# Down projection of a gated ConvFFN by seven block products, with weight sums formed in device memory

## The chip, the cores and the metric

One core of a Trainium2 chip runs the whole program. The engines spoken of are PE (TensorE: matmuls, and PEld for the loading of their stationary operand), DVE (VectorE), ACT (ScalarE), POOL (GpSimd) and SP (SyncE, which here only issues transfers). The metric is the time on the device in microseconds (us), the median of the runs shown; lower is better. A profile is one execution recorded by the hardware profiler.

## The reference, cut to what matters

The program is one layer of a decoder trunk, for 1024 positions of width 1024, in float32. `@` is a matrix product.

```python
h = layer_norm(x, ln_in_g, ln_in_b)
u = h @ w_in                                  # 1024 x 1024 @ 1024 x 9248
u_glu, z, xbc, dt_raw, gate_a, gate_b = split_in(u)
y_a = conformer_branch(u_glu, ...)            # depthwise conv of 31 taps, norm, product
y_b = ssd_branch(z, xbc, dt_raw, ...)         # Mamba-2 in chunks of 128 positions
mix = (sigmoid(gate_a) * y_a + sigmoid(gate_b) * y_b) @ w_o
h = layer_norm(ALPHA * h + mix, ln1_g, ln1_b)

def conv_ffn(h, w_up, dw_w, dw_b, w_down):
    u = causal_dwconv(h @ w_up, dw_w, dw_b)   # up: 1024 x 1024 @ 1024 x 5632, 3 taps
    gate, val = split(u, 2, axis=-1)          # 2816 columns each
    return (silu(gate) * val) @ w_down        # down: 1024 x 2816 @ 2816 x 1024

h = layer_norm(ALPHA * h + conv_ffn(h, ...), ln2_g, ln2_b)
```

## The kernel before

**Precision.** Each float32 operand of a large product is split into a rounded part and a remainder: `A.copy` on ACT makes the first, a subtraction on DVE the second (`weights`, L144 to L153, for a tile that comes from memory; `split_pair`, L723 to L728, for a tile at hand). A product of two split operands is three matmuls (`mm3`, L158 to L163). Weight tiles are 128 x 1024 and pass through three staging buffers (`wst`, tag "st") and three split buffers (`wsp`, tag "w"). All transfers are issued on SP, in one order that a scheduler fixes when the program is built; so is the order of each engine.

**Stages.** The positions are worked in two halves of 512 (`hh`). For each half: `ln_in`, `mixers`, `combine`, and an output projection. In `mixers(hh)` a loop over four groups `g` makes six columns of the input projection (`column`), the gate tiles `zs` (`z_gate`: four tiles, written by ACT at L443), two GLU tiles (`glu`, for which `conv31` does 30 taps each on DVE at L415), and then the chunks of 128 positions of the SSD branch (`ssd_group`). There, for each of four chunks, POOL multiplies the tile `au` at L473 into a single buffer, and two matmuls at L482 read it. So POOL can make the next `au` only when PE has read the last one, and PE goes on to the next chunk only when the next `au` is there. At the end of each half `combine` sums on POOL (L611, L613, L624).

**Up projection.** `ffn_blocks` cuts h into blocks (early and late positions, first and second half of the width) and forms sums of blocks; the product with the up weights is done as seven block products in place of eight. `up_first` does two of them for a pair of tiles and stores the results in device memory; `up_rest` does the other five for each `j` of 22. The weight sums that these need are formed on DVE in `up_weights` (four subtractions or additions of 128 x 512, L823 to L826), from two tiles loaded at L818 and L820. `up_rest` ends with the taps, the gate and a store of the activated tile (128 channels x 1024 positions) at L882.

**Down projection.** `down(hh)` takes the 22 activated tiles and the 22 weight tiles of one half of the positions: for each `k` it loads a weight tile of 128 x 1024 and an activation tile of 128 x 512, splits both, and does eight blocks of three matmuls into eight accumulators: 22 x 8 x 3 matmuls for a half and 1056 in all. The last four tiles are done position by position so that the layer norm of one (`ln_out`) runs beside the matmuls of the next.

Of the kernel before, what the change touches and what calls it, by code (L numbers as in the profile page):

```python
# [16 lines left out]
P = 128  # L17
D = 1024
# [37 lines left out]
def kernel(  # L56
# [82 lines left out]
    act_scr = [dram.tile([P, T], F32, name=f"act_scr{j}") for j in range(NF)]  # L139
# [4 lines left out]
    def weights(src, name, pl=None, eng=None, bufs=None):  # L144
# [8 lines left out]
        return w  # L153

# [400 lines left out]
    def mixers(hh, hT):  # L555
        pre = first_columns(hh, hT, (CT_DT, CT_B, CT_C))
        with pool(f"mixers{hh}") as pl:
            time_steps(pl, hh, pre[0])
            for g in range(GROUPS):
# [5 lines left out]
                zs = z_gate(pl, hh, hT, g)  # L565
                vs = [(i, glu(pl, hh, hT, i)) for i in (2 * g, 2 * g + 1)]
# [163 lines left out]
    def ffn_blocks(tp, qp, mixT):  # L730
# [33 lines left out]
        def block_sums(t):  # L764
# [9 lines left out]
            e.tensor_tensor(out=t1, in0=t0, in1=raw[:, 0:4, ts], op=ALU.subtract)  # L774
            V.tensor_tensor(out=t0, in0=b22, in1=t0, op=ALU.subtract)
            parts(lambda i: sums[0][:, i, :, ts], b22)
            V.tensor_tensor(out=t2, in0=b22, in1=t1, op=ALU.subtract)
            parts(lambda i: sums[2][:, i, :, ts], t2)
            parts(lambda i: sums[1][:, i, :, ts], t1)
            e.tensor_tensor(out=t2, in0=raw[:, 4:8, ts], in1=t2, op=ALU.subtract)  # L780
# [20 lines left out]
    def up_first(qp, bl, j):  # L801

        w = weights(wup[j], f"ue{j}")
        ps = bank(1)
        product(ps, lambda i: w[:, i, 0:HALF], bl["b11"], True)
        s1 = qp.tile([P, HALF], F32, tag="s1", bufs=2, name=f"s1_{j}")
# [3 lines left out]
        c11 = qp.tile([P, HALF], F32, tag="c11", bufs=2, name=f"c11_{j}")  # L810
        A.copy(c11, ps)
        SY.dma_start(first_scr[j][1], c11)

    def up_weights(upp, j):

        with tc.high_priority(offset=2000):
            r1 = upp.tile([P, D], F32, tag="raw", bufs=3, name=f"ra{j}")
            SY.dma_start(r1, wup[j])  # L818
            r2 = upp.tile([P, D], F32, tag="raw", bufs=3, name=f"rb{j}")
            SY.dma_start(r2, wup[NF + j])  # L820
            a11, a12, a21, a22 = r1[:, :HALF], r1[:, HALF:], r2[:, :HALF], r2[:, HALF:]
            s3 = upp.tile([P, HALF], F32, tag="s3", name=f"s3_{j}")
            V.tensor_tensor(out=s3, in0=a11, in1=a21, op=ALU.subtract)  # L823
# [5 lines left out]
            w3 = split_pair(upp, s3, f"s3_{j}", HALF, 2)  # L829
        return w24, w10, w3  # L830

    def up_rest(upp, bl, j):
# [17 lines left out]
        V.tensor_tensor(out=uv[:, late], in0=uv[:, late], in1=pc_, op=ALU.add)  # L850
# [3 lines left out]
        V.tensor_tensor(out=uv[:, 2 : 2 + HALF], in0=s, in1=pc_, op=ALU.add)  # L854
        os = []
        for jj, u in ((j, ug), (NF + j, uv)):
            o = upp.tile([P, T], F32, tag="o", bufs=2, name=f"fo{jj}")
# [24 lines left out]
        SY.dma_start(act_scr[j], ov)  # L882

    def down(upp, dp, hh, g, b):

        LAST, OWN = 4, 2
        pss = [[bank(1), bank(0)] for _ in range(4)]
        ws, acts = {}, {}
        hs = slice(hh * HALF, (hh + 1) * HALF)

        def load(k):
            own = k >= NF - OWN
            ws[k] = weights(wdown[k], f"dn{hh}_{k}", dp if own else None, bufs=OWN if own else None)
            with tc.high_priority(offset=2000):
                raw = upp.tile([P, D], F32, tag="raw", bufs=3, name=f"ar{hh}_{k}")[:, :HALF]
                SY.dma_start(raw, act_scr[k][:, hs])
                if hh == 0 and k < 2:
                    acts[k] = split_pair(upp, raw, f"act{hh}_{k}", HALF, 2)
                else:
                    acts[k] = split_pair(dp, raw, f"act{hh}_{k}", HALF, 4, "act")  # L900

        def block(k, t, q):
            mm3(
                pss[t][q],
                lambda i: acts[k][:, i, t * P : (t + 1) * P],
                lambda i: ws[k][:, i, q * HALF : (q + 1) * HALF],
                k == 0,
                k == NF - 1,
            )

        for k in range(NF - LAST):
            load(k)
            for t in range(4):
                for q in range(2):
                    block(k, t, q)
        rs = []
        for t in range(4):
            r = dp.tile([P, D], F32, tag="r", bufs=4, name=f"rf{hh}_{t}")
            SY.dma_start(r, h1_scr[(4 * hh + t) * P : (4 * hh + t + 1) * P, :])
            rs.append(r)  # L920
        for k in range(NF - LAST, NF):
            load(k)
        for t in range(4):
            for q in range(2):
                for k in range(NF - LAST, NF):
                    block(k, t, q)
                r = rs[t][:, q * HALF : (q + 1) * HALF]
                V.scalar_tensor_tensor(
# [146 lines left out]
```

## Time and profile before

| | |
|---|---|
| median of 3 runs | 2039.78 us (2038.25 to 2040.18) |
| the profiled execution, time | 2041.08 us |
| the profiled execution, span of its trace | 2039.3 us |
| granted PE clock, mean | 0.996 |
| busy: PE, PEld, DVE, ACT, POOL | 98%, 81%, 81%, 48%, 7% of the span |
| transfers | 278.24 MB on one queue, 40.3% of 16 engines |

The span runs from the first to the last instruction. A busy PE is not a PE at its peak: matmuls overlap, so the distance from one start to the next is what each costs, and not its duration. The stages of the first half of the positions lie at about 0 to 700 us, those of the second half at 700 to 1400, the up projection at 1400 to 1785 and the down projection from 1785.2 to the end. A row of the timeline has the start in us, the duration in us, the engine, the line, the operation and its tiles; "x6" are six instructions merged in one row. A row of the table of stretches has for each engine its busy us and the number of instructions, then the granted PE clock, the busy share of the transfer engines, and GB/s.

### The profile page before, as it was taken

Reading aid. Unit: us, or ns where it says so; the run is one execution under the profiler, and the core shown is the slowest. Engines: PE = TensorE matmul, PEld = TensorE weight load, DVE = VectorE, ACT = ScalarE, POOL = GpSimd, SP = SyncE. Lnnn points to the kernel's source line nnn. Section 1 sums busy time; section 2 is a strip of 40 time slices with the busy share of each in tenths; the row PEclk is TensorE's granted clock in tenths of the full one; section 3 lists DMA queues with packets and bytes.
Section 4 is the critical chain, followed back from the end, with each engine's and each line's share of the span. In section 5 each row is a group of like instructions: output and inputs, shape, how many; then the busy total and the mean of one; then the engine's idle time right before and its main releaser. Section 6 shows DMA issues by size and latency. Waiting matters only on the chain.

```text
span 2039.3 us, 24778 instructions
## 1 busy us (share of the span) xinstructions
PE 2000.0 (98%) x9296; PEld 1650.1 (81%) x9296; DVE 1654.7 (81%) x2185; ACT 973.0 (48%) x1392; POOL 148.0 (7%) x125
## 2 busy tenths in 40 slices
PE   7999999999999999999999999999999999999998
PEld 6888887888788888888888888877888888888886
DVE  7599999989766869999998976586888888853736
ACT  4465654556453356665454635354444444433231
POOL 2010101001400000100100130010000000000000
PEclk9999999999999999999999999999999999999999
DMA  6222223333436522222323353566454444464542
GB/s 218 93 69 88 86 94 104 99 103 114 158 121 213 209 88 77 90 84 76 126 88 104 109 171 128 195 217 217 155 164 157 164 165 156 160 227 149 209 159 83
DMA packets 95015, 279.81 MB, mean 137 GB/s; under 512 B 10800, under 2 KB 10800, under 8 KB 94896
## 3 DMA queue, kind: packets, MB, share of 16 engines
q1 hardware_dynamic: 94896, 278.24, 40.3%
q8 instruction: 73, 1.20, 0.2%
q14 instruction: 46, 0.38, 0.1%
HBM read 229.96 MB, written 48.23 MB: 136 GB/s over the span
## 4 chain that ended last, share of the span: by engine, by line
PE 69%; DVE 23%; issue 4%; DMA 2%; ACT 1%; SPq 0%; POOL 0%; DVEq 0%; ACTq 0%
PE acc L163 15%; PE acc L161 15%; PE acc L162 15%; DVE c L415 8%; PE sm L161 6%; PE sm L163 6%; PE sm L162 6%; DVE xbc L370 2%; PE acc L352 1%; PE sm L529 1%; PE sm L510 1%; DVE w_so L150 1%; DVE w_z L150 1%; DVE w_c L150 1%; PE sm L187 1%
## 5 line engine op out<-in xcount | busy, mean ns | idle before, releaser
L415 DVE SCALAR_TENSOR_TENSOR c<-v,pc,c 128x512 f32<-128x512 f32 x480 | 375.3, 805 | 7.2 <-ACT c L404 5.8
L473 POOL TENSOR_TENSOR au<-seg_mv,head_of 128x1024 fp32r<-128x1024 f32 x32 | 77.6, 2425 | 961.8 <-PE sm L482 728.8
L161 PE MATMUL acc<-hT,w_c 128*128 128x512 f32 x352 | 141.0, 400 | 0.0
L162 PE MATMUL acc<-hT,w_c 128*128 128x512 f32 x352 | 140.6, 399 | 0.0
L163 PE MATMUL acc<-hT,w_c 128*128 128x512 f32 x352 | 138.4, 393 | 0.0
L150 DVE TENSOR_TENSOR w_dn<-st_dn,w_dn 128x1024 fp32r<-128x1024 f32 x44 | 53.4, 1222 | 104.2 <-ACT w_dn L149 104.2
L370 DVE SCALAR_TENSOR_TENSOR xbc<-u,pc,xbc 128x512 f32<-128x512 f32 x144 | 109.8, 774 | 0.7 <-ACT xbc L368 0.5
L161 PE MATMUL sm<-h1s,w_s 128*128 128x512 f32 x264 | 103.5, 392 | 6.0 <-DVE fuv L848 3.1
L149 ACT CAST w_dn<-st_dn 128x1024 fp32r<-128x1024 f32 x44 | 46.0, 1053 | 131.6 <-PE sm L163 115.4
L162 PE MATMUL sm<-h1s,w_s 128*128 128x512 f32 x264 | 102.8, 389 | 0.0
L163 PE MATMUL sm<-h1s,w_s 128*128 128x512 f32 x264 | 102.1, 389 | 0.0
L162 PE MATMUL acc<-w_z,hT 128*128 128x512 f32 x256 | 100.8, 394 | 0.0
L161 PE MATMUL acc<-w_z,hT 128*128 128x512 f32 x256 | 100.8, 401 | 0.0
L163 PE MATMUL acc<-w_z,hT 128*128 128x512 f32 x256 | 100.7, 396 | 0.0
L149 ACT CAST w_c<-st_c 128x1024 fp32r<-128x1024 f32 x50 | 52.5, 1051 | 86.9 <-PE acc L163 66.2
L162 PEld LDWEIGHTS acc<-hT,w_c 128*128 128x128 f32 x352 | 66.1, 188 | 16.9 <-issue 3.8
L163 PEld LDWEIGHTS acc<-hT,w_c 128*128 128x128 f32 x352 | 66.1, 188 | 16.1 <-issue 2.6
L161 PEld LDWEIGHTS acc<-hT,w_c 128*128 128x128 f32 x352 | 66.1, 188 | 15.9 <-issue 2.6
L150 DVE TENSOR_TENSOR w_c<-st_c,w_c 128x1024 fp32r<-128x1024 f32 x47 | 60.6, 1289 | 20.2 <-ACT w_c L149 20.2
L163 PE MATMUL acc<-h1b,w_ue 128*128 128x512 f32 x176 | 68.5, 391 | 2.0 <-DVE w_ue L150 2.0
L161 PE MATMUL acc<-h1b,w_ue 128*128 128x512 f32 x176 | 68.7, 391 | 1.1 <-ACT s L807 0.7
L163 PE MATMUL sm<-h1b,w_s 128*128 128x512 f32 x176 | 69.2, 393 | 0.0
(312 smaller groups left out, 5741.8 us busy)
## 6 DMA issues: line engine op xcount, KB each, us to landing
st_c<-wcol SPq DMA_DIRECT2D x50, 512.0 KB, 3.5
st_dn<-wdown SPq DMA_DIRECT2D x44, 512.0 KB, 3.6
st_z<-wz SPq DMA_DIRECT2D x32, 512.0 KB, 3.4
st_wo<-wo SPq DMA_DIRECT2D x24, 512.0 KB, 3.9
st_ue<-wup SPq DMA_DIRECT2D x22, 512.0 KB, 4.1
ra<-wup SPq DMA_DIRECT2D x22, 512.0 KB, 3.8
rb<-wup SPq DMA_DIRECT2D x22, 512.0 KB, 3.5
act_scr<-fo SPq DMA_DIRECT2D x22, 512.0 KB, 2.7
```

The lines of the kernel that those rows point to most:

```text
L149: A.copy(w[:, 0, :], st)
L150: (eng or V).tensor_tensor(out=w[:, 1, :], in0=st, in1=w[:, 0, :].bitcast(F32), op=ALU.subtract)
L161: TE.matmul(ps, wa(0), xa(0), start=start, stop=False, skip_group_check=more)
L162: TE.matmul(ps, wa(0), xa(1), start=False, stop=False, skip_group_check=more)
L163: TE.matmul(ps, wa(1), xa(0), start=False, stop=stop, skip_group_check=more)
L187: TE.transpose(pt[:, i * P : (i + 1) * P], src[:, (q + i) * P : (q + i + 1) * P], ident)
L352: TE.matmul(ps[:, ts], w[:, i, k * P : (k + 1) * P], hT[:, j, k, ts], start=n == 0 and k == 0, stop=n == 2 and k == KD - 1,)
L370: V.scalar_tensor_tensor(out=o, in0=u[:, k : k + HALF], scalar=pc[:, wc + k : wc + k + 1], in1=o, op0=ALU.mult, op1=ALU.add,)
L415: V.scalar_tensor_tensor(out=accs[i], in0=v[:, k : k + HALF], scalar=pc[:, wc + k : wc + k + 1], in1=accs[i], op0=ALU.mult, op1=ALU.add,)
L473: G.tensor_tensor(out=au, in0=seg_mv[:, c, :].unsqueeze(1).to_broadcast([P, 8, P]), in1=head_of[:, g, :].unsqueeze(2).to_broadcast([P, 8, P]),
L510: TE.matmul(po, CT[:, cs], S, start=True, stop=True)
L529: TE.matmul(py[:, hs], m[:, h, :], xs[:, hs], start=True, stop=True)
```

## The change: what it does

The down projection is cut into blocks as the up projection was: early and late positions, first and second half of the 2816 channels, first and second half of the 1024 outputs. It becomes seven block products of 11 steps each, and a step is 4 blocks of three matmuls: 7 x 11 x 4 x 3 = 924 matmuls. Each step loads 128 x 512 of a weight block, or of a sum of weight blocks, and 128 x 512 of an activation block or sum (two transfers into one tile), and splits them together. The sums of activation blocks are formed on DVE in `up_rest`, for each second `j`, and stored.

The sums of weight blocks, for the up and for the down projection, are no longer formed on DVE: they are formed in device memory during `mixers`. For each sum three transfers are issued: on SP one float from a `zs` tile into the destination (so that the sum waits until that tile is there), on SP a copy of the first block over it, and on POOL a transfer that adds the second block to it. `sum_some` issues them after `z_gate` of each group, so that each set of sums takes three groups to form. The host orders the tiles of the up weights so that the two tiles of one set of sums are `wup[4*c : 4*c+4]`, taken with a step of two; the source of such a transfer therefore counts 2 x 128 rows of 512 floats, and its destination 256 rows of 512 floats.

```diff
+    def sum_weights(a11, a12, a21, a22, s1, s2, s3, s4):
+        yield ((s1, a21, a22), (s3, a11, a21))
+        yield ((s2, s3, a22),)
+        yield ((s4, s2, a12),)
+    def sums_up(c):
+        s24, s1, s3 = up_sums[c]
+        w = wup[4 * c : 4 * c + 4].rearrange("(n i) p d -> i n p d", i=2)
+        blocks = (w[i, :, :, q * HALF : (q + 1) * HALF] for i in range(2) for q in range(2))
+        return sum_weights(*blocks, s1, s24[:, :, :HALF], s3, s24[:, :, HALF:])
+    def sums_down(c):
+        n = min(2, NK - 2 * c)
+        blocks = (
+            wdown[k : k + n, :, q * HALF : (q + 1) * HALF]
+            for q in range(2)
+            for k in (2 * c, NK + 2 * c)
+        )
+        return sum_weights(*blocks, *(s[:n] for s in down_sums[c]))
+    to_sum = [sums_up(c) for c in range(NK)] + [sums_down(c) for c in range((NK + 1) // 2)]
+    def sum_some(n, zs):
+        for i, steps in enumerate(to_sum[max(0, 3 * n - 6) : 3 * n + 3]):
+            after = zs[i % len(zs)]
+            for dst, first, then in next(steps):
+                SY.dma_start(dst[0, 0:1, 0:1], after[0:1, 0:1])
+                SY.dma_start(dst, first)
+                G.dma_start(dst, then, accum_op=ALU.add)
...
                 zs = z_gate(pl, hh, hT, g)
+                sum_some(4 * hh + g, zs)
                 vs = [(i, glu(pl, hh, hT, i)) for i in (2 * g, 2 * g + 1)]
...
     def up_weights(upp, j):
+        s24, s1, s3 = (t[j % 2] for t in up_sums[j // 2])
...
-            SY.dma_start(r1, wup[j])
-            SY.dma_start(r2, wup[NF + j])
-            V.tensor_tensor(out=s3, in0=a11, in1=a21, op=ALU.subtract)
-            V.tensor_tensor(out=a21, in0=a21, in1=a22, op=ALU.add)
-            V.tensor_tensor(out=a11, in0=a21, in1=a11, op=ALU.subtract)
-            V.tensor_tensor(out=a12, in0=a12, in1=a11, op=ALU.subtract)
+            SY.dma_start(r1, s24)
             w24 = split_pair(wsp, r1, f"s24_{j}")
+            SY.dma_start(r2[:, :HALF], s1)
+            SY.dma_start(r2[:, HALF:], wup[2 * j + 1, :, HALF:])
             w10 = split_pair(wsp, r2, f"s10_{j}")
+            SY.dma_start(r3[:, :HALF], s3)
...
-        SY.dma_start(act_scr[j], ov)
+        if j < NK:
+            SY.dma_start(b11_scr[j], ov[:, early])
+            return ov
+        SY.dma_start(b2_scr[j - NK], ov)
+        a, b, t = before, ov, og
+        V.tensor_tensor(out=t[:, early], in0=a[:, late], in1=b[:, late], op=ALU.subtract)
+        V.tensor_tensor(out=a[:, late], in0=a[:, early], in1=a[:, late], op=ALU.subtract)
+        V.tensor_tensor(out=t[:, late], in0=t[:, early], in1=a[:, early], op=ALU.subtract)
+        V.tensor_tensor(out=a[:, early], in0=b[:, early], in1=t[:, late], op=ALU.add)
+        SY.dma_start(t32_scr[j - NK], t)
+        SY.dma_start(t41_scr[j - NK], a)
...
+    def down(upp, dp, g, b):
+        def load(p, k, w_of, x_of):
...
+                pl, tag = ((wst, "st"), (upp, "raw"))[n_steps % 2]
+                st = pl.tile([P, D], F32, tag=tag, bufs=3, name=f"dr{p}_{k}")
+                SY.dma_start(st[:, :HALF], w_of(k))
+                SY.dma_start(st[:, HALF:], x_of(k))
...
+        products = (
+            (X, True, plain(0, E), acts(b11_scr), one),
+            (Y, True, plain(1, E), acts(b2_scr), two),
+            (X, False, summed(2), acts(t32_scr, L), six),
+            (Y, True, summed(3), acts(t32_scr), seven),
+            (X, False, summed(1), acts(t41_scr, L), five),
+            (Y, False, plain(1, L), acts(t41_scr), four),
+            (X, False, summed(4), acts(b2_scr, L), three),
+        )
+        for p, (banks, first, w_of, x_of, then) in enumerate(products):
+            end = NK - LAST if p == 6 else NK
+            for k in range(end):
+                w = load(p, k, w_of, x_of)
+                for t in range(4):
+                    block(banks[t], w, t, first, k)
...
+    up_order = [i * NF + h * (NF // 2) + k for k in range(NF // 2) for h in range(2) for i in range(2)]
...
+        "wup": flat(cols(a["w_ffn_up"][0]))[up_order],
```

The signs of some block sums in `ffn_blocks` and `up_rest` change with the order of the sums; their number and shapes stay.

More of the change, by code (lines that the diff above doesn't have):

```diff
@@ L881, in up_rest @@
         )
-        SY.dma_start(act_scr[j], ov)
[L884 to L902, printed above, removed]
-            mm3(
[L904 to L908, printed above, removed]
-            )
-        for k in range(NF - LAST):
-            load(k)
-            for t in range(4):
[L914 to L928, printed above, removed]
-                    out=r, in0=r, scalar=ALPHA, in1=pss[t][q], op0=ALU.mult, op1=ALU.add
-                )
-            ln_out(upp, 4 * hh + t, rs[t], g, b)
@@ L974 @@
     g, b = row(dp, RW_2G, D, "ln2_g"), row(dp, RW_2B, D, "ln2_b")
-    for hh in range(2):
-        down(upp, dp, hh, g, b)
+    down(upp, dp, g, b)
 _OUT = "out_0_dram"
```

102 lines of the change are left out of this document (83 added, 19 removed).

## The prediction

> **What bounds the kernel now.** I read the page's totals and its chain of waits first, then the stretches of 50 us, and last the order of time around the gates.
>
> ```profile
> span 2039.3 us, 24778 instructions
> ...
> PE 2000.0 (98%) x9296; PEld 1650.1 (81%) x9296; DVE 1654.7 (81%) x2185; ACT 973.0 (48%) x1392; POOL 148.0 (7%) x125
> ...
> PE 69%; DVE 23%; issue 4%; DMA 2%; ACT 1%; SPq 0%; POOL 0%; DVEq 0%; ACTq 0%
> ```
>
> PE is busy all the time and holds 69% of the chain; DVE's 23% is mostly the long convolution, which runs beside it. So a matmul less is time saved, and anything that makes PE stand still is time added.
>
> ```profile
> 200.00:250.00 50.00, 50.00 (x242) 40.87 (x241) 50.00 (x70) 34.42 (x61) 6.86 (x3) 1.00 0.24 79
> 1300.00:1350.00 50.00, 48.89 (x236) 40.41 (x235) 36.32 (x45) 26.37 (x36) 0.00 (x0) 1.00 0.70 242
> 1650.00:1700.00 50.00, 49.23 (x217) 40.47 (x216) 42.86 (x50) 21.94 (x24) 0.50 (x5) 1.00 0.45 151
> 1850.00:1900.00 50.00, 50.00 (x222) 41.38 (x222) 20.39 (x24) 15.76 (x19) 0.00 (x0) 1.00 0.46 155
> ```
>
> In the mixers (first row) PE and DVE are both full and the transfer engines lie three quarters idle. In the up projection (third) PE misses 0.77 us of 50. In the down projection (fourth) PE is full: 222 matmuls of one form in 50 us, 0.2252 us each.
>
> **Part 1, matmuls removed.** 1056 become 924: 132 x 0.2252 = 29.7 us less, in a stage where PE alone sets the time. This is the one gain of size.
>
> **Part 2, the feeding of the down projection.**
>
> ```profile
> L149 ACT CAST w_dn<-st_dn 128x1024 fp32r<-128x1024 f32 x44 | 46.0, 1053 | 131.6 <-PE sm L163 115.4 <-DMA st_dn<-wdown 16.3
> L150 DVE TENSOR_TENSOR w_dn<-st_dn,w_dn 128x1024 fp32r<-128x1024 f32 x44 | 53.4, 1222 | 104.2 <-ACT w_dn L149 104.2
> ```
>
> A step is 12 matmuls, 2.70 us, and needs one such cast (1.05 us) and one subtraction (1.22 us): each fits. It also needs 524 KB, 194 GB/s, where 242 GB/s was reached above. SP issues two transfers a step. I count nothing; if the loads fail to keep up, a tenth of the 208 us is 20 us, a rival below. The last layer norm stays as it is.
>
> **Part 3, DVE in the up projection.**
>
> ```profile
> L823 DVE TENSOR_TENSOR s<-ra,rb 128x512 f32<-128x512 f32 x22 | 15.2, 689 | 11.9 <-issue 7.0 <-DMA rb<-wup 4.8
> L161 PE MATMUL sm<-h1s,w_s 128*128 128x512 f32 x264 | 103.5, 392 | 6.0 <-DVE fuv L848 3.1 <-ACT w_s L726 2.9
> ```
>
> Four operations of this form (0.69 us) go from each of 22 tiles, 61 us, and four come to each of 11 pairs, 30 us. DVE is 43 of 50 us busy there, so this is off the path. At best the 6.0 us that PE waited go; I count 0 and keep 6 for the range.
>
> **Part 4, the transfers that form the sums.** This decides the sign. There are 68 sums: 44 for up, 24 for down, each with a one-float transfer and a copy on SP and an adding transfer on POOL. Most copies and all additions have 256 rows of 2 KB. But 22 copies on SP and all 44 additions for the up sums read the host's tiles, whose source counts 2 x 128 rows and whose destination counts 256. No transfer in the profile has such a form; all have 128 rows outermost on both sides.
>
> ```profile
> q1 hardware_dynamic: 94896, 278.24, 40.3%
> ...
> st_c<-wcol SPq DMA_DIRECT2D x50, 512.0 KB, 3.5
> ...
> act_scr<-fo SPq DMA_DIRECT2D x22, 512.0 KB, 2.7
> ...
> out_dram<-rf SPq DMA_DIRECT2D x16, 256.0 KB, 2.1
> ```
>
> One engine moves 278.24 MB / (0.403 x 16 x 2039.3 us) = 21.2 KB a us while busy. The 512 KB of st_c land in 3.5 us, which two engines could not do (12.4 us): rows outermost are dealt over many engines. If the 256 rows are too, a copy takes 1.55 us. If the outermost count of 2 sets how many engines share it, each of two moves 262 KB in 12.4 us; by the slope of the two stores (256 KB more in 0.6 us, 27 KB a us an engine), 9.6 us. The nearest rows are 128-row transfers, dealt by their outermost count; I carry that rule over and take 12.4 us, with 1.55 us as the other end.
>
> The Trainium skill ("DMA: Bandwidth & Descriptors", section "Why a DMA increments its semaphore by 16 and not by 1") says that a transfer runs on the largest number of engines up to 16 that divides the slowest counts of both sides, and that SP's take the lowest-numbered ones: by it these copies run on two engines, always the same two, and the sum is the one below. No run shows it yet.
>
> What stands behind them: in SP's order of the changed program six such copies follow the first gate tile of groups 0, 1 and 2 of the first half, and four that of group 3. The weight tile after them needs all its engines, so it lands after them (taking each engine to work SP's transfers in order). On POOL the additions stand between the `au` of one chunk and that of the next, and each waits for its copy: so the next `au` waits for the last copy.
>
> ```profile
> L149 ACT CAST w_c<-st_c 128x1024 fp32r<-128x1024 f32 x50 | 52.5, 1051 | 86.9 <-PE acc L163 66.2 <-issue 8.6 <-PE acc L352 6.8
> L150 DVE TENSOR_TENSOR w_c<-st_c,w_c 128x1024 fp32r<-128x1024 f32 x47 | 60.6, 1289 | 20.2 <-ACT w_c L149 20.2
> L473 POOL TENSOR_TENSOR au<-seg_mv,head_of 128x1024 fp32r<-128x1024 f32 x32 | 77.6, 2425 | 961.8 <-PE sm L482 728.8 <-DVE seg_mv L323 232.9
> ```
>
> ```profile
> 81.22 29.83 SPq L147 DMA_DIRECT2D st_c<-wcol  x6
> 81.24 1.09 ACT L443 ACTIVATE zs<-acc 128x512 f32<-128x512 f32 x2
> 107.16 0.39 PE L161 MATMUL acc<-hT,w_c 128*128 128x512 f32 x1
> 112.62 0.39 PE L161 MATMUL acc<-hT,w_c 128*128 128x512 f32 x1
> ...
> 175.18 1.58 ACT L443 ACTIVATE zs<-acc 128x512 f32<-128x512 f32 x3
> 218.11 0.47 PE L482 MATMUL sm<-au,seg_st 128*128 128x512 f32 x1
> ...
> 270.26 1.58 ACT L443 ACTIVATE zs<-acc 128x512 f32<-128x512 f32 x3
> 319.09 0.61 PE L467 MATMUL sm<-ident,xbc 128*128 128x128 f32 x4
> ...
> 414.59 0.60 ACT L443 ACTIVATE zs<-acc 128x512 f32<-128x512 f32 x1 [1.14 <-PE acc L163]
> 468.38 1.89 PE L529 MATMUL sm<-xs,m 128*128 128x64 f32 x16
> ```
>
> The wait for the gate itself costs little: behind SP's first one-float transfer stands a weight load (`st_c`, issued at 81.22 before), and the tile is there at 81.8. The later waits on SP are each for a one-float transfer that lies behind a copy; the weight loads queued there wait for these, and PE for the loads.
>
> - Group 0: the gate tile is there at 81.8 us, the first copy starts about 2 us later (2.1 us for the small transfer), six end at 84 + 74 = 158. The second weight tile behind the gate was loaded ahead before; now it lands at 160 to 161 and is split (1.05 + 1.29 us) at 163. PE wants it at 112.6: 51 us.
> - Group 1: started at 178, six copies and three spread ones (1.55 us, of sums already begun) end at 258; the additions' issue and `au` (2.4 us) make 263. PE wants that `au` at 218.1: 45 us.
> - Group 2: from 273, six copies, six spread ones and weight loads between them: 361, `au` at 365; in the new order of PE it is wanted right behind the transposes of 319.09, at 320: 45 us. Inside this, a weight tile is late by some 24 us.
> - Group 3: from 417, four copies, six spread ones and two of down: 479; the weight tile behind them is usable at 484, and wanted just ahead of the row of 468.38: 16 us.
>
> The sum is 157 us. With 9.6 us for a copy the same steps give 34 + 28 + 27 + 6 = 95. The additions come on top: each reads two streams, so 12 to 25 us on its engines; where one falls on the two engines of the copies, it stretches the queue. Of 37 in the first half I take none in the sum and up to four a group, 100 us in all, for the upper end. In the second half no copy on SP has the odd form: nothing is counted.
>
> **Sum.** 2041.1 (the profiled execution; its span is 1.8 us shorter, and the median of the runs 1.3 us below it) - 29.7 + 157 = 2168, and against the median 2039.8 - 29.7 + 157 = 2167. I say 2167.
>
> **The rivals.**
> - Faster: the 256 rows are spread. Then a set of six copies takes 9 us and some 2 us each for the small ones, ends by 105, and nothing above is late (the `au` wanted next at 119, the weight at 110). For it: the share of 24% in the mixers leaves room, and all 128-row transfers spread. Against: the form of the source. 2039.8 - 29.7 = 2010, 2000 to 2025. It decides below about 4 us a copy: six then end at 108, as the weight is wanted.
> - The transfers are spread, but the gain is lost: SP waits at each gate tile while weight loads stand behind it, 68 adding transfers keep POOL, and the down projection at 194 GB/s loses a tenth (20 us). 2010 + 20 + 10 = 2040, 2030 to 2065. Against: SP's waits now are for free buffers, which have slack.
>
> **How the numbers follow.** The forecast (two engines) has 0.78, within 2060 to 2300: below, 2039.8 - 29.7 - 6 + 95 less a third of it; above, 2167 + 100 and some 30 for restarts. Spread and faster has 0.16, spread and lost 0.06 (0.02 of it no change). Faster 0.16, same 0.02, slower 0.82, against 0.2%, 4 us, which is about what a measurement of this kernel can tell. The range 2045 to 2300 holds nearly all of the first and half of the third case: 0.8.
>
> **What would show it.** Right: the transfers of the odd form take 9 us and more to land, and those of 256 rows on both sides 2 to 4; PE waits for DVE's split or for `au` by tens of us in four places between 100 and 500 us, and none of that size between 780 and 1190; the down projection takes about 215 us in place of 245. Wrong: these transfers land in 3 to 5 us, or the second weight tile behind the gate arrives ahead of them; then the time is near 2010. A mis-sized part 4 would show as the copy's own time: each us more or less on it moves the sum by 22 us.

## The result, and the profile after

| | before | after |
|---|---|---|
| median of 4 runs each, us | 2039.01 (2036.23 to 2040.18) | 2320.68 (2319.00 to 2323.03) |
| ratio | 1 | 1.1384 (95% interval 1.1365 to 1.1404) |
| span of the profiled execution, us | 2039.3 | 2321.3 |
| mean granted PE clock | 0.996 | 0.930 |

The change makes the kernel 13.8% slower. The forecast was slower, at 2167 us with an upper end of 2300; the loss is 282 us where 127 were foretold.

The page of the kernel after: totals, queues, chain.

```profile
span 2321.3 us, 25094 instructions
...
PE 1990.7 (86%) x9164; PEld 1638.3 (71%) x9164; DVE 1641.6 (71%) x2142; ACT 983.4 (42%) x1381; POOL 251.7 (11%) x193
...
q1 hardware_dynamic: 129092, 333.04, 42.8%
q0 software_dynamic: 96832, 35.24, 10.3%
...
PE 65%; DVE 9%; issue 8%; DMA 8%; SPq 7%; POOL 2%; ACT 1%; DVEq 0%; POOLq 0%; ACTq 0%
```

PE has 132 matmuls less and stands still for 2321.3 - 1990.7 = 331 us, where it stood for 39 before. In the chain, "issue", DMA and SP's queue have come in; none of them held more than 4% before. The queue q0 is new: the adding transfers.

Where PE stands: stretches of the kernel before (first fence) and after (second). A group comes later when those ahead of it are slower, so each stretch runs from the first gate tile of a group (`zs`, on ACT) to that of a later one: groups 0, 1 and 2 of the first half, then its group 3 with the end of that half, then groups 0 to 2 of the second half together.

```profile
81.20:175.20 94.00, 94.00 (x442) 76.53 (x441) 80.77 (x107) 57.03 (x93) 9.41 (x4) 1.00 0.24 79
175.20:270.30 95.10, 95.10 (x466) 78.73 (x465) 95.06 (x134) 57.39 (x96) 6.86 (x3) 1.00 0.26 86
270.30:414.60 144.30, 143.36 (x686) 117.53 (x686) 143.12 (x197) 74.12 (x125) 12.10 (x5) 1.00 0.32 103
414.60:751.70 337.10, 331.90 (x1578) 275.55 (x1577) 256.53 (x350) 162.18 (x228) 33.01 (x18) 0.99 0.43 146
751.70:1084.20 332.50, 332.04 (x1590) 272.50 (x1589) 318.30 (x435) 185.69 (x284) 27.92 (x12) 1.00 0.28 91
```

```profile
82.20:247.20 165.00, 97.71 (x444) 78.19 (x443) 80.17 (x107) 56.86 (x92) 21.29 (x10) 0.79 0.33 84
247.20:408.60 161.40, 99.31 (x457) 80.22 (x457) 94.31 (x132) 57.06 (x95) 23.45 (x12) 0.80 0.45 110
408.60:638.70 230.10, 151.02 (x692) 122.19 (x692) 144.56 (x199) 74.77 (x125) 33.96 (x17) 0.82 0.48 121
638.70:1026.60 387.90, 335.85 (x1578) 278.45 (x1578) 252.02 (x350) 162.22 (x228) 52.38 (x30) 0.93 0.54 159
1026.60:1396.80 370.20, 337.63 (x1591) 275.47 (x1590) 317.27 (x435) 185.27 (x284) 60.65 (x39) 0.95 0.58 153
```

PE's busy time taken from each stretch leaves 67, 62, 79, 52 and 33 us idle after, against 0, 0, 1, 5 and 0 before. The transfer engines are on average no more than six tenths busy meanwhile, and move at most 159 GB/s where 242 were reached before: the loss is not one of total bandwidth. The granted clock falls with the idle time.

PE's waits in the kernel after:

```profile
PE sm L528 <- POOL au L519: 103.7, 4, 40.4
PE acc L207 <- ACT w_c L161: 65.8, 2, 61.7
PE acc L207 <- ACT w_so L161: 38.5, 1, 38.5
PE sm L564 <- ACT bt L552: 38.1, 3, 32.4
PE sm L528 <- DVE state L566: 26.0, 2, 25.5
```

Two kinds were foretold and are there: a late weight (`w_c`, `w_so`; and `state`, which stands on DVE behind the split of a late weight) and a late `au`, behind the additions on POOL. A third was not: `bt` stands on ACT behind an operation of the convolution, and that waited for a store of the convolution's tile, which SP issues among the copies:

```profile
315.43 0.81 ACT L450 ACTIVATE c<-v,pc 128x512 f32<-128x512 f32 x1 [30.92 <-DMA c_scr<-c]
```

Group 0 closely, by the order of time of SP (first fence) and of POOL (second; start, duration, what it did, and the idle time before with what ended it):

```profile
89.84 8.99 SPq L197 DMA_DIRECT2D up_s<-zs  x1
98.92 54.28 SPq L198 DMA_DIRECT2D up_s<-wup  x4
153.25 12.26 SPq L159 DMA_DIRECT2D st_c<-wcol  x3
```

```profile
97.51 2.06 POOL L199 DMA_DIRECT2D up_s<-wup  x1 [23.47 <-DMA up_s<-wup]
116.97 1.90 POOL L199 DMA_DIRECT2D up_s<-wup  x1 [17.40 <-DMA up_s<-wup]
140.46 1.88 POOL L199 DMA_DIRECT2D up_s<-wup  x1 [21.59 <-DMA up_s<-wup]
151.53 1.90 POOL L199 DMA_DIRECT2D up_s<-wup  x1 [9.19 <-DMA up_s<-wup]
162.19 1.88 POOL L199 DMA_DIRECT2D up_s<-wup  x1 [8.76 <-DMA up_s<-wup]
173.20 1.88 POOL L199 DMA_DIRECT2D up_s<-wup  x1 [9.12 <-DMA up_s<-wup]
174.28 2.72 POOL L519 TENSOR_TENSOR au<-seg_mv,head_of 128x1024 fp32r<-128x1024 f32 x1
```

POOL issues an addition when its copy has landed, so the distances are the copies' own times: 19.5, 23.5, 11.1, 10.7 and 11.0 us. The last three answer to the 12.4 us of the prediction; the second and third copy were on their way while the first additions ran. SP is busy from 98.92 to 153 us with issuing four copies: the issue itself stands, for 54 us, and the weight loads stand behind it.

### The profile page after: what moved, and what is told of

The parts are those of the page before. It is cut to its first block, busy times and chain, and to the rows that moved or that the text cites. A ratio compares the mean times of both kernels' runs of the same rounds, so it can differ in the third digit from the quotient of the medians.

```text
span 2321.3 us, 25094 instructions
## 1 busy us (share of the span) xinstructions
PE 1990.7 (86%) x9164; PEld 1638.3 (71%) x9164; DVE 1641.6 (71%) x2142; ACT 983.4 (42%) x1381; POOL 251.7 (11%) x193
## 2 busy tenths in 40 slices
DMA packets 226048, 369.87 MB, mean 159 GB/s; under 512 B 93765, under 2 KB 93765, under 8 KB 225733
## 3 DMA queue, kind: packets, MB, share of 16 engines
q0 software_dynamic: 96832, 35.24, 10.3%
## 4 chain that ended last, share of the span: by engine, by line
PE 65%; DVE 9%; issue 8%; DMA 8%; SPq 7%; POOL 2%; ACT 1%; DVEq 0%; POOLq 0%; ACTq 0%
PE acc L209 14%; PE acc L207 14%; PE acc L208 14%; PE sm L209 5%; PE sm L207 5%; PE sm L208 5%; SPq L198 5%; DMA st_c<-wcol 3%; DVE c L461 2%; PE sm L575 1%; PE acc L398 1%; DMA c_scr<-c 1%; POOL up_s L199 1%; DVE xbc L416 1%; DMA up_s<-up_s 1%
## 5 line engine op out<-in xcount | busy, mean ns | idle before, releaser
L461 DVE SCALAR_TENSOR_TENSOR c<-v,pc,c 128x512 f32<-128x512 f32 x480 | 367.1, 787 | 52.7 <-ACT c L450 51.3
L207 PE MATMUL acc<-hT,w_c 128*128 128x512 f32 x352 | 144.1, 409 | 65.8 <-ACT w_c L161 65.8
L208 PE MATMUL acc<-hT,w_c 128*128 128x512 f32 x352 | 143.9, 409 | 0.0
L209 PE MATMUL acc<-hT,w_c 128*128 128x512 f32 x352 | 143.5, 408 | 0.0
L774 DVE TENSOR_TENSOR w_dn<-dr,w_dn 128x1024 fp32r<-128x1024 f32 x77 | 93.7, 1222 | 67.0 <-ACT w_dn L773 64.0
L528 PE MATMUL sm<-au,seg_st 128*128 128x512 f32 x64 | 28.0, 450 | 129.8 <-POOL au L519 103.7
L199 POOL DMA_DIRECT2D up_s<-wup x44 | 83.4, 1913 | 480.7 <-issue 171.3
L773 ACT CAST w_dn<-dr 128x1024 fp32r<-128x1024 f32 x77 | 80.8, 1055 | 118.3 <-DMA dr<-t_scr 35.0
L207 PEld LDWEIGHTS acc<-hT,w_c 128*128 128x128 f32 x352 | 68.3, 194 | 83.8 <-ACT w_c L161 66.6
L528 PEld LDWEIGHTS sm<-au,seg_st 128*128 128x128 f32 x64 | 12.2, 197 | 132.4 <-POOL au L519 104.7
L536 ACT ACTIVATE m<-sm 128x512 f32<-128x512 f32 x64 | 37.6, 596 | 134.5 <-PE sm L528 134.2
L207 PE MATMUL acc<-yT,w_so 128*128 128x512 f32 x128 | 53.5, 423 | 38.6 <-ACT w_so L161 38.5
```

The costliest lines, as they stand in the source:

```text
L199: G.dma_start(dst, then, accum_op=ALU.add)
L207: TE.matmul(ps, wa(0), xa(0), start=start, stop=False, skip_group_check=more)
L208: TE.matmul(ps, wa(0), xa(1), start=False, stop=False, skip_group_check=more)
L209: TE.matmul(ps, wa(1), xa(0), start=False, stop=stop, skip_group_check=more)
L461: V.scalar_tensor_tensor(out=accs[i], in0=v[:, k : k + HALF], scalar=pc[:, wc + k : wc + k + 1], in1=accs[i], op0=ALU.mult, op1=ALU.add,)
L773: A.copy(w[:, 0, :], src)
```

## The experiments

All are edits of the changed kernel. "Spread" means that a transfer has 128 or 256 rows outermost on both sides. Four kernels leave work out, and their time is read as a part's price: the one without additions keeps only the first block of each sum, the one with small additions adds 8 rows of each 128, and the two without sums read plain weight blocks in the place of sums.

| run | us, median | ratio to before (interval) |
|---|---|---|
| e3_no_sums | 2011.12 | 0.9859 (0.9844 to 0.9874) |
| e6_small_adds | 2020.62 | 0.9907 (0.9892 to 0.9923) |
| e1_spread | 2097.97 | 1.0283 (1.0254 to 1.0312) |
| e11_both_split | 2087.45 | 1.0240 (1.0220 to 1.0261) |
| e8_gates_first | 2125.01 | 1.0418 (1.0394 to 1.0442) |
| e2_no_adds | 2191.73 | 1.0744 (1.0722 to 1.0765) |
| e5_adds_spread | 2291.70 | 1.1235 (1.1200 to 1.1270) |
| e4_copies_spread | 2310.73 | 1.1327 (1.1301 to 1.1353) |
| e15_half_odd_adds | 2124.45 | 1.0423 (1.0400 to 1.0446) |
| e14_no_sums_tail | 2008.09 | 0.9853 (0.9840 to 0.9867) |
| e13_down_only_tail | 2033.05 | 0.9976 (0.9965 to 0.9987) |
| e7_down_only | 2035.23 | 0.9979 (0.9969 to 0.9989) |
| e12_acts_on_pool | 2045.50 | 1.0025 (1.0014 to 1.0037) |
| e9_up_on_pool | 2065.04 | 1.0137 (1.0118 to 1.0156) |
| e10_all_on_pool | 2091.63 | 1.0261 (1.0246 to 1.0277) |

**No sums.** What the seven products bring by themselves.

```diff
-                sum_some(4 * hh + g, zs)
...
-            SY.dma_start(r1, s24)
+            SY.dma_start(r1, wup[2 * j])
```

> No sums are formed at all: the products that used them read plain blocks of the weights, of the same size. This is the price of the rest of the change. The prediction's parts 1 to 3 give 2040 - 30 = 2010 us. If the down projection's loads or the new sums on DVE cost something of their own: 2025 us and more.

It took 2011.12 us, 27.9 less than the kernel before. So everything above it, 2320.7 - 2011.1 = 309.6 us, is the price of the transfers that form the sums. Against this run PE in the changed kernel idles 286 us more (331 against 2009.6 - 1964.6 = 45), and its 9164 matmuls, the same in number, are busy for 26 us longer (1990.7 against 1964.6).

**No additions.**

```diff
-                G.dma_start(dst, then, accum_op=ALU.add)
```

> The additions on POOL are left out (the sums are then only their first block), copies and one-float transfers stay as they are. Theory A with the copies as its main part: six copies of 10.9 us in a row still hold the weight loads back in groups 0 to 2, some 100 us of standing PE in the first half and none in the second: 2110 to 2140 us. If the additions carry most of the loss: under 2060 us.

2191.73 us, above both cases: the copies with their gates cost 180.6 us, the additions on top of them 129.0. The same five stretches in this kernel, from gate tile to gate tile:

```profile
81.70:221.40 139.70, 97.35 (x444) 77.99 (x443) 78.66 (x107) 56.84 (x92) 9.78 (x4) 0.85 0.22 76
221.40:369.80 148.40, 97.40 (x463) 80.23 (x462) 95.20 (x134) 57.15 (x96) 6.35 (x3) 0.82 0.26 87
369.80:561.90 192.10, 151.66 (x687) 122.09 (x686) 142.91 (x197) 74.19 (x124) 11.82 (x5) 0.88 0.33 110
561.90:927.10 365.20, 335.52 (x1579) 277.39 (x1578) 255.03 (x350) 162.20 (x228) 32.41 (x18) 0.95 0.44 152
927.10:1264.10 337.00, 332.88 (x1589) 272.28 (x1588) 318.90 (x435) 184.77 (x284) 28.39 (x12) 1.00 0.39 130
```

PE is idle for 42, 51, 40, 30 and 4 us. The copies cost time in all four groups of the first half, with the transfer engines less than half busy. The additions add 25, 11, 39 and 22 us there, and make nearly all of the 33 us in the second half.

How many engines a copy holds can be read in group 0, where only copies run while PE stands (first fence, without additions). In the kernel after, one addition is under way beside the copies from 104 to 116 us (second fence):

```profile
120.00:138.00 18.00, 0.00 (x0) 0.00 (x0) 0.00 (x0) 0.00 (x0) 0.00 (x0) 0.50 0.13 51
```

```profile
104.00:116.00 12.00, 9.71 (x45) 7.69 (x43) 0.00 (x0) 0.00 (x0) 0.00 (x0) 1.00 0.14 33
```

A share of 0.13 of 16 engines is 2.1 engines, and 51 GB/s is 10.3 us for 512 KB: two engines carry a copy. With the addition the share is the same and the rate lower, so these two transfers had the same two engines.

**All sums spread**, by another order of the host's tiles:

```diff
-        w = wup[4 * c : 4 * c + 4].rearrange("(n i) p d -> i n p d", i=2)
+        w = wup[4 * c : 4 * c + 4].rearrange("(i n) p d -> i n p d", i=2)
```

> The host puts the two tiles of a pair of sums next to each other, so that the source of each copy and each addition counts 256 rows like its destination; the work and the order of PE, DVE and ACT are those of the changed kernel. Theory A (the form of 2 x 128 rows puts a transfer on two engines, and that is the whole loss): the 512 KB copies land in 2 to 4 us and the time is 2010 to 2030 us. Rival B (68 sums of three transfers each in the mixers are too much for SP's and POOL's queues in any form): still above 2150 us. Rival C (additions are slow in any form, some 30 us, as the median of 32 us for the down sums has it): between, 2050 to 2150.

2097.97 us, within the third case. PE, DVE and ACT have the same instructions in the same order and the transfers move the same blocks, and 222.7 of the 309.6 us are gone. 86.9 remain, so the kernel is still slower than before. Of its longer span PE stands for 59 us (104.2 against 45.0 without sums), and its matmuls are busy for 29 us longer (1993.9 against 1964.6). To see that it is the form, and not the host's order, each transfer was cut in two in the host's old order, each part with its own gate:

```diff
-                SY.dma_start(dst[0, 0:1, 0:1], after[0:1, 0:1])
-                SY.dma_start(dst, first)
-                G.dma_start(dst, then, accum_op=ALU.add)
+                for m in range(dst.shape[0]):
+                    SY.dma_start(dst[m, 0:1, 0:1], after[0:1, 0:1])
+                    SY.dma_start(dst[m], first[m])
+                    G.dma_start(dst[m], then[m], accum_op=ALU.add)
```

> The host's order of the tiles stays as in the changed kernel; each copy and each addition is issued as two transfers of 128 rows, each with its own one-float gate. If the form of the transfer (two engines for an outermost count of 2) is what makes the difference between 2321 and 2098, this comes out near 2098: 2085 to 2130, with something for twice the number of issues. If the host's order itself did it, near 2290 to 2320.

2087.45 us: the form it is.

**Copies alone spread, additions alone spread.**

```diff
-                SY.dma_start(dst, first)
+                for n in range(dst.shape[0]):
+                    SY.dma_start(dst[n], first[n])
```

> Each copy is issued as two transfers of 128 rows, the additions keep the form of 2 x 128 rows. If the loss is the copies' (they stand in SP's queue ahead of the weight loads): 2040 to 2080 us, what is left being the additions' (28 us on two engines each). If the additions are the loss: above 2150 us, little below the changed kernel.

```diff
-                G.dma_start(dst, then, accum_op=ALU.add)
+                for n in range(dst.shape[0]):
+                    G.dma_start(dst[n], then[n], accum_op=ALU.add)
```

> Each addition is issued as two transfers of 128 rows; the copies keep the form that two engines carry. Kernels measured so far: copies in the odd form and no additions 2192 us, copies spread and odd additions 2311, both odd 2321, both spread 2098. If the odd additions are what was mis-sized and the odd copies add their 180 us alone, this comes to 2192 plus what spread additions cost, at most the 87 us that stay in the spread form: 2190 to 2280. If either form alone is enough to keep the two engines and the queues behind them full, so that the parts overlap, it comes out like its mirror image, near 2310.

2310.73 and 2291.70 us, against 2320.68 with both odd and 2097.97 with both spread. Either odd form alone brings nearly the whole loss: the parts don't add up, and the expectation that additions were the one culprit fell in the second run. (In the first, the second half of each copy has no gate, and the order of SP put these early, from 11 us on.) The adding transfers by their issue rows, with the median us to landing last: the kernel after, all spread, and copies alone spread, in this order.

```profile
up_s<-wup POOLq DMA_DIRECT2D x44, 512.0 KB, 31.8
down_s<-wdown POOLq DMA_DIRECT2D x20, 512.0 KB, 32.1
```

```profile
q0 software_dynamic: 17984, 34.61, 9.5%
...
up_s<-wup POOLq DMA_DIRECT2D x44, 512.0 KB, 13.3
down_s<-wdown POOLq DMA_DIRECT2D x20, 512.0 KB, 13.0
```

```profile
up_s<-wup POOLq DMA_DIRECT2D x44, 512.0 KB, 28.8
down_s<-wdown POOLq DMA_DIRECT2D x20, 512.0 KB, 31.7
```

An odd addition takes 29 to 32 us to land, a spread one 13. The down sums' additions have no odd form anywhere, and take 32 us as well where odd ones run, so an odd addition makes others late. The packets of the adding queue, 10.3% of 16 engines after, are 3825 us. If each of the 24 down sums has the 47 us of the spread kernel (3189 us, 9.5% there, over 68), 61 are left for an odd one, and on two engines that is 31 us: an estimate, but it agrees with the landing.

**Half of the odd additions.** Is there a price for each, or a queue that fills?

```diff
+                if (n + i) % 2:
+                    G.dma_start(dst, then, accum_op=ALU.add)
+                else:
+                    for m in range(dst.shape[0]):
+                        G.dma_start(dst[m], then[m], accum_op=ALU.add)
```

> All copies and half of the additions of the up sums as transfers of 128 rows, each with its own gate; 22 of the 44 additions keep the odd form. With none odd it was 2087 us, with all 44 odd (and the copies spread) 2311. If each odd addition costs its own time on the engines it holds, the loss is in proportion: 2180 to 2215. If a few that are under way at a time are enough to hold back every load, it saturates: 2250 to 2310. If the 44 only build up a queue when they are dense, half of them cost little: 2100 to 2150.

2124.45 us, 37 above the kernel with all split. (19 of the 44 additions had the odd form, three fewer than the expectation says.) The first 19 cost 1.9 us each, the other 25 make up the rest to 2311, 7.5 us each. That is the last of the three cases, a queue that builds up where they are dense; the queue itself was not seen.

**Small additions**, in the kernel with all sums spread. What are the 87 us that stay?

```diff
-                G.dma_start(dst, then, accum_op=ALU.add)
+                G.dma_start(dst[:, 0:8], then[:, 0:8], accum_op=ALU.add)
```

> The kernel with all sums spread (2098 us), each addition cut to 8 of the 128 rows of each tile (the rest of a sum is left as its first block): its issue, its place on POOL and its waits stay, its bytes nearly go. Theory: the 87 us that are left above the kernel without sums (2011) come from the bytes of the additions, which share all engines with the weight loads in the stretches where the transfer engines were 0.8 to 1.1 busy: then about 2020 to 2045. Rival: they come from SP, which stands at each gate and each copy with weight loads queued behind it: then 2080 to 2100.

2020.62 us: 77 of the 87 us go with the bytes of the additions. All 68 copies, all gates, all issues and all waits together cost 9.5 us when the copies are spread. The queue's row above tells why the bytes are dear: 9.5% of 16 engines over 2098.1 us are 3189 us of engine time for 34.61 MB, 10.9 KB a us, where the copying queue moves 21.

**Gates first.** All one-float transfers of a group ahead of all its copies:

```diff
+        for after, dst, _, _ in todo:
+            SY.dma_start(dst[0, 0:1, 0:1], after[0:1, 0:1])
+        for _, dst, first, then in todo:
+            SY.dma_start(dst, first)
+            G.dma_start(dst, then, accum_op=ALU.add)
```

> The kernel with all sums spread, but in each group all one-float transfers are issued first and the copies after them, so that SP stands for one of their latencies and not for each. If SP's standing is what is left of the loss, some 9 waits of 2 us in each of four groups fall together: 2098 less 30 to 70 us, 2030 to 2068. If the bytes of copies and additions are what is left, the same bytes come in a tighter burst: 2090 to 2115.

2125.01 us, slower by 27 and above both ranges. SP's standing at each gate was not the loss; that it kept the bytes apart is the likeliest reading.

**Toward a version that beats both.** The up sums go back to DVE, only the 24 down sums are formed by transfers, four or fewer for each group over both halves:

```diff
-    to_sum = [sums_up(c) for c in range(NK)] + [sums_down(c) for c in range((NK + 1) // 2)]
+    to_sum = [sums_down(c) for c in range((NK + 1) // 2)]
...
-        for i, steps in enumerate(to_sum[max(0, 3 * n - 6) : 3 * n + 3]):
+        for i, steps in enumerate(to_sum[max(0, n - 2) : n + 1]):
```

> A version meant to beat both: only the 24 sums of the down weights are formed by transfers, one new set for each group over both halves; the sums of the up weights are formed on DVE as in the kernel before (four operations of 128 x 512 for each tile). The down projection's 29.7 us stay saved. If the loss is in the number of sums in a group and in the form of the up sums' transfers, what stays is 24 of 68 sums thinly spread: 2011 plus 3 us of PE in the up projection plus 0 to 15, so 2012 to 2030. If any such transfer between the weight loads costs PE its share of the 87 us, 24/68 of it is 31: 2045, as slow as before.

2035.23 us, 0.2% under the kernel before, with an interval that excludes 1; it lies between the two ranges, 24 us above the kernel without sums. More than half of that goes in the up projection. The stretch from 1500 to 1600 us without sums (first fence) and in this version (second):

```profile
1500.00:1600.00 100.00, 100.00 (x443) 82.85 (x442) 81.58 (x91) 43.44 (x47) 1.09 (x11) 1.00 0.60 200
```

```profile
1500.00:1600.00 100.00, 96.41 (x422) 78.58 (x420) 90.72 (x109) 43.20 (x46) 1.10 (x11) 1.00 0.54 175
```

DVE is 91 of 100 us busy where it was 82, and PE misses 3.6, in a stage of 385 us. So DVE's work was taken to POOL in three ways: the four sums of the up weights (`V.tensor_tensor` to `G.tensor_tensor` in `up_weights`); these, and the down sums too in place of the adding transfers, in the up projection; and only the four sums of activation blocks.

> As the version with only the down sums as transfers (2035 us), but the four operations of the up sums go from DVE to POOL, which does nothing in the up projection. That version's PE was 96.4 of 100 us busy between 1400 and 1800, where the kernel without sums had 99.5 to 100: some 13 us. If DVE's load was the reason, they come back: 2018 to 2026. If the wait was for the sums themselves (a longer chain from load to split), POOL, which is slower for each operation, makes it worse: 2035 to 2050.

> No adding transfers at all: the up sums on POOL as in the run before this, and the down sums on POOL too, during the up projection, from weight tiles loaded into the staging buffers that are little used there, and stored. Transfers in that stage grow by 2 MB for each pair of tiles, from some 165 to 225 GB/s. If only the transfers in the mixers cost what is left of the loss, 2011 to 2018. If the transfer engines are too full in the up projection (242 GB/s was the most seen in 50 us there), loads come late: 2025 to 2050.

> As the version with only the down sums as transfers (2035 us), with the four sums of activation blocks of each pair of tiles on POOL in place of DVE. They are wanted only in the down projection, so their latency costs nothing; DVE loses 44 operations of 0.68 us, 30 us of the up projection's 385. If DVE's load is what costs that version 13 us there: 2022 to 2030. But POOL took 2.1 us for each operation of this form beside a busy DVE, and DVE's split took 1.7 in place of 1.2 us beside it: if that slowing outweighs the load taken off, 2035 to 2045.

None came in as hoped: 2065.04, 2091.63 and 2045.50 us; the first two lie above both of their ranges. The first of them by groups of instructions on POOL (mean ns last before the bar), then one group of DVE in the down-only version and in this one:

```profile
L861 POOL TENSOR_TENSOR rc<-ra,rb 128x512 f32<-128x512 f32 x22 | 51.8, 2354 | 109.1 <-DVE w_s L764 55.4 <-DMA rb<-wup 46.8 <-DMA s<-first_scr 6.9
L862 POOL TENSOR_TENSOR rb<-rb 128x512 f32<-128x512 f32 x22 | 45.7, 2078 | 1.6
...
L661 POOL TENSOR_TENSOR var<-var,csq 128x512 f32<-128x512 f32 x14 | 22.6, 1617 | 13.6 <-ACT csq L660 12.6
```

```profile
L904 DVE SCALAR_TENSOR_TENSOR fo<-fuv,pc,fo 128x1024 f32<-128x1024 f32 x44 | 56.4, 1281 | 0.0
```

```profile
L904 DVE SCALAR_TENSOR_TENSOR fo<-fuv,pc,fo 128x1024 f32<-128x1024 f32 x44 | 76.3, 1734 | 0.2
```

POOL takes 1.8 to 2.4 us for each of the four operations (two are shown), where one of this form takes it 1.6 elsewhere and DVE 0.69; they stand one after the other between the load and the split; and DVE's own operations get longer beside it. That DVE's load alone is the price was wrong; what share the longer chain has and what share the slowing was not tried apart, nor what the larger transfers cost in the second of the three.

**The end.** From the last matmul to the end it is longer than before (the rows stand in the next section). The last seven steps position by position in place of four, without sums and in the down-only version:

```diff
-        LAST = 4
+        LAST = 7
...
-                first = n_steps < 3
+                first = n_steps < 3 or n_steps >= 7 * NK - 3
```

> The kernel without sums (plain weight blocks in the place of sums, 2011 us), with the last seven steps of the last product done position by position in place of the last four; the last three of them use the three split buffers that are free by then. After the last matmul DVE still has 19.4 us of layer norms in that kernel, against 9.3 in the kernel before. A position of four steps is 4 x 3 x 0.2252 = 2.7 us of PE, and DVE needs some 5 us for its layer norm, so it falls behind by 2.3 us at each of three; with seven steps a position is 4.7 us. If that is where the tail comes from: 2011 less 6 to 8, 2003 to 2005. If the split weights of seven steps are not there in time, or the tail is made by the four layer norms of the product before it: 2009 to 2020.

> The same edit in the version with only the down sums formed by transfers (2035 us): 2027 to 2029 if the tail shortens as in the kernel without sums; 2033 to 2045 if not.

2008.09 us, 3.0 less, and 2033.05, 2.2 less than the same without it: some of the tail, less than hoped. In the first, 16.2 us are left after the last matmul (2004.8 - 1988.6) of 19.4, and DVE works through them without a pause: it is still at the layer norms of the product before when the last ones come. The down-only version with this edit is the fastest of those that leave no work out, 0.24% under the kernel before (0.13 to 0.35%); the difference to the one without the edit is within their spreads.

## Why the prediction was wrong in size

**Part 1 was right.** The matmuls of the down projection, from the first to the last, before and after.

```profile
1785.20:2030.00 244.80, 244.80 (x1081) 202.55 (x1079) 122.75 (x164) 73.81 (x97) 0.00 (x0) 1.00 0.48 168
```

```profile
2086.70:2301.80 215.10, 215.08 (x949) 177.80 (x947) 138.19 (x152) 86.11 (x86) 0.00 (x0) 1.00 0.60 197
```

215.1 us, after as without sums, as "about 215 in place of 245" said: 29.7 less, and PE full. One reading behind it was off, though nothing hung on it: of DVE's 23% of the chain the page gives the long convolution (L415) 8%, which is not most of it.

**Part 2 was right on the loads and wrong on the end.** PE misses 0.02 us at 197 GB/s, so the rival in which the down projection loses a tenth is out. But "the last layer norm stays as it is" failed: from the end of these rows to the end of the span it was 9.3 us before, 19.5 after and 19.4 without sums (from 1990.2 to 2009.6). All eight layer norms now come in the last product and behind it, where four were done at half time before, and DVE ends after PE by 10 us more.

**Part 3 was undersized, and hid it.** 0 with up to 6 us was counted; without sums the down projection begins 10.1 us earlier. So 10 us are won ahead of it and 10 lost behind, and the 27.9 us of the run without sums agree with the 29.7 of the sum partly by chance.

**Part 4, the copies: the form was right, the size came out in part by luck.** The copies in the odd form alone cost 180.6 us, 157 were foretold. That two engines carry such a copy was taken from a row that could not show it; the runs bear it out: a share of 0.13 of 16 engines, and most of the loss goes when only the form is changed. The Trainium skill ("DMA: Bandwidth & Descriptors", section "Why a DMA increments its semaphore by 16 and not by 1") has it as its rule, the largest number up to 16 that divides the slowest counts of both sides; the times of the copies and the run with both transfers split agree.

By groups, 51, 45, 45 and 16 us stand against 42, 51, 40 and 25 in the kernel without additions (30 less the 5 of before). But a copy took 10.3 us there and not 12.4, and for that the prediction's own scale, 95 us at 9.6 and 22 for each us more, gives some 110: an estimate. The rest came from what no step held. In group 1 PE was to wait for an `au` behind the additions; this kernel has none, and PE stood for 51 us because a store of the convolution landed late, and ACT and then DVE waited for it:

```profile
297.65 0.81 ACT L449 ACTIVATE c<-v,pc 128x512 f32<-128x512 f32 x1 [52.39 <-DMA c_scr<-c]
```

And its matmuls were busy for 18 us longer than without sums (1982.6 against 1964.6). Whether "22 us for each" is the price of a us was not tried.

**Part 4, the additions: this step failed.** "Of 37 in the first half I take none in the sum and up to four a group, 100 us in all, for the upper end", and "In the second half ... nothing is counted." The additions cost 129.0 us on top of the copies. They were mis-sized in three places:
- the price: 12 to 25 us on two engines, measured 29 to 32 to landing;
- the count: none stood in the sum, and they add 25, 11, 39 and 22 us of idle time in the four groups of the first half. That they do so by holding engines which the weight loads and stores need is argued; one addition on the copies' two engines is shown above;
- the second half: nothing was counted, and PE is idle for 33 us there, 4 without additions. The mark "none of that size between 780 and 1190" was missed, as a wait between 1050 and 1200 us shows (first fence). Only seven of the additions there have the odd form, and the form is not what costs: with all sums spread 28 us stay in the same stretch (second fence), and with small additions 4. It is the bytes.

```profile
PE sm L528 <- POOL au L519: 19.1, 1, 19.1
```

```profile
802.10:1170.70 368.60, 340.27 (x1591) 276.86 (x1590) 314.43 (x435) 185.27 (x284) 53.17 (x39) 0.95 0.57 154
```

A fourth thing was in no step of the sum, and in the upper end only as "some 30 for restarts": the clock. Matmuls were priced at 0.2252 us throughout, but behind a long wait PE has half its clock for some us. After the 40 us wait for `au` in the kernel after, 13 matmuls took 5.5 us, 0.42 us each:

```profile
541.80:547.30 5.50, 5.43 (x13) 4.32 (x14) 2.48 (x3) 4.03 (x8) 0.02 (x1) 0.50 0.58 106
```

The same 9164 matmuls were busy for 26 us longer after than without sums.

**The rivals.** "Spread" as a fact of this kernel was wrong, and its time for the spread form, 2010, was wrong as well: it is 2098, because it too held the additions at nothing. The rival of spread transfers with the gain lost named SP's gates, POOL's issues and the down projection at 30 us; the small additions show all of SP's and POOL's part at 9.5 us, and the bytes at 77.

**What stays open.** That either odd form alone brings nearly the whole loss goes with a queue that builds up, and so does it that 19 of the 44 odd additions cost a sixth of what all cost; no run shows the queue itself. Which two engines an addition holds is not settled: the records don't name the engine of a packet. The first of group 0 had those of the copies, but the fourth to sixth copies took 11 us each while additions ran, so not every one has.

## What to carry to other kernels

Price a transfer by engine time and not by bytes over the total rate, and look at the outermost counts of both of its sides: with an outermost 2, 512 KB took 10 to 11 us here and held back loads on otherwise idle transfer engines. Ask for each transfer that is queued behind, stores too, what waits for it. An adding transfer is not a copy: here it moved half as much for each us of engine time, and 68 of them cost 77 us in the spread form. Work that is taken from a busy engine to a transfer queue or to POOL still needs a price in the stage where it lands; and a term whose bound is wide (here 0 to 100 us) should not stand in the sum as zero.

## What the hardware did that was not expected

- SP's issue of a transfer can stand for tens of us: 54.28 us for four copies in group 0 after, with the weight loads queued behind.
- In the odd form an addition brings many small packets: the page counts 93765 packets under 512 B after, and 15224 with all sums spread. And its issue takes POOL 1.9 us, against 0.88 spread.
- POOL and DVE are slower beside each other: POOL's 128x512 operation takes 1.8 to 2.4 us in place of 1.6, DVE's row above 1.73 in place of 1.28. The Trainium skill ("SBUF — State Buffer", section "SBUF: two separate sides") names a port pair that the two share and that one holds for a whole instruction, where a DVE operation with two inputs from that memory meets a GpSimd operation that reads it; the rows agree in direction, and none shows a whole block.
- The clock that PE is granted falls with its waits, to 0.79 in the first group, and stays at 0.50 for the first 5.5 us of work in the row above. The Trainium skill ("TensorE: Matmul & The Clock Gate", section "Part 1: The HAM clock gate") says that an idle PE is gated to half its clock and gets it back after some us of work; the mean clock of 0.930 over a run that idles 14% of its span agrees.
